# Three of sixteen output projection blocks as 32-bit products and as narrower halves in a streaming encoder layer

## The chip, the cores and the metric

The kernel runs on one core of a Trainium2 chip. The metric is the device time of one execution in microseconds (us). Before the change it is 1701.15 us, the median of three runs (1701.06 to 1701.47).

The engines of the core that matter here are TensorE (PE, matmuls; its weight loads have a row of their own, PEld), VectorE (DVE), ScalarE (ACT), GpSimd (POOL) and SyncE (SP), whose queue issues the loads from memory.

## The reference: what is computed

One layer of a streaming encoder for two request groups, 256 new positions of a prompt and 64 of a running stream, that share one set of weights. The two groups lie side by side as T = 320 columns, so each weight is read once. Cut to what matters:

```python
def layer(x, ...):                      # x: (B, T, 2048)
    xn = rmsnorm(x, norm_mix[l])
    proj = xn @ w_in[l]                 # q, k, v, u, vs, gates
    ...                                 # stick-breaking attention a, spatial gate bb
    gates = jax.nn.sigmoid(g + b_gate[l])
    g_a, g_b = gates[..., :D_MODEL], gates[..., D_MODEL:]
    merged = g_a * (a @ w_branch_a[l]) + g_b * (bb @ w_branch_b[l])
    h = x + merged @ w_out[l]           # the output projection: 2048 x 2048
    hn = rmsnorm(h, norm_ffn[l])
    gu = hn @ w_gate_up[l]
    h = h + (jax.nn.silu(gu[..., :D_FF]) * gu[..., D_FF:]) @ w_down[l]
    return h, k, v, vs
```

All inputs are 32-bit floats. The change touches `merged @ w_out` alone.

## The kernel before

Features lie on the 128 partitions and the 320 positions on the free axis. Each projection is cut into blocks of 128 output features. A block sums products over chunks of 128 input features into one accumulator `acc` in PSUM (three buffers), 128 x 320 of 32 bits.

**Products in halves.** Each 32-bit operand is kept as two tiles of the type `fp32r`: a high part, rounded, and a low part, the rest. For an activation these are pairs such as (`mh`, `ml`); for a weight they are `wh` and `wl`. `product` (lines 80 to 85) issues three matmuls for each 128 x 128 weight tile: high weight by high activation (L83), high weight by low activation (L84), low weight by high activation (L85), each over 320 columns. Each matmul has its own weight load.

**Weights.** `weights` (line 68) loads 128 x 1024 of a weight matrix (512 KB, eight tiles, half of a block with 16 tiles) into `raw` (three buffers) through SP's queue. ACT casts it to `wh` (L75), and DVE subtracts to get `wl` (L76); `wh` and `wl` have four buffers each. `block` (line 87) does this twice for an output block and issues 2 x 8 x 3 = 48 matmuls.

**The stage around the change.** The loop that merges the branches runs over m = 0 to 15. Its last round ends with the blocks of `w_a` and `w_b`; DVE multiplies them with the gates (L647, L649), adds them (L650), ACT casts the sum to `mh` (L653) and DVE subtracts to get `ml` (L654). The 16 pairs (`mh`, `ml`) are the list `merged`. Then the output projection runs over m = 0 to 15: a load of 128 x 320 of x into `xr` (two buffers, L662, kept in program order on SP), `block(w_out[m], merged)`, the residual add on DVE (L664, `h`), the scaled halves of the result for the next stage (L125 on ACT, L126 on DVE), and the sum of squares (ACT and POOL). The feed-forward stage follows.

**What sets the order.** Each engine works through its instructions in the order in which a scheduler put them when the program was built; DMAs of a queue are issued in order too. A tile's next use of a buffer waits until the last reader of the old content is done. The tag `B` has 32 buffers of 128 x 320. Up to the last round of the merge loop they hold the halves of both branches (`aT`, `bT`), and in the feed-forward stage the activations.

Products of full 32 bits, without halves, occur before the change only in the attention and gating parts, with 1, 64 or 128 columns: for instance L416 (128 columns), L488 (`wt` by `av` 128, `wt` by `cv` 64), L604 (128) and L728 (1 column). L418 and L488 with tiles `B` are products of halves over 256 columns, and L421 over 320. The first products, L243, are halves over 320 columns as well.

Of the kernel before, what the change touches and what calls it, by code (L numbers as in the profile page):

```python
# [8 lines left out]
F32 = mybir.dt.float32  # L9
F32R = mybir.dt.float32r  # L10
AF = mybir.ActivationFunctionType
ALU = mybir.AluOpType

P = 128
TP = 256
TS = 64
T = TP + TS
D = 2048
KD = D // P
H = 8  # L20
HALF = 8
# [12 lines left out]
def stream_step(ctx: ExitStack, tc: tile.TileContext, xT, w_in, w_a, w_b, w_out, w_gu, w_down,  # L34
                gains, ws_t, bs, ck_t, cv, y_t, k_t, v_t, sv_t):
    nc = tc.nc
    pool = lambda name, bufs=1, **kw: ctx.enter_context(tc.tile_pool(name=name, bufs=bufs, **kw))
    const = pool("const")
    wraw = pool("wraw", 3)
# [5 lines left out]
    def acc():  # L45
        return psum.tile([P, 512], F32, tag="acc", bufs=3, name="acc")
# [15 lines left out]
    def tick():  # L62
        state["tick"] += 1
        for fn, a in later.pop(state["tick"], ()):
            fn(*a)


    def weights(src, n, view=lambda t: t):
        raw = wraw.tile([P, HALF * P], F32, tag="raw", name="raw")
        d = nc.sync.dma_start(out=view(raw[:, : n * P]), in_=src)  # L70
        if state["tick"] < 4:
            tc.keep_in_program_order(d)
        wh = wsplit.tile([P, HALF * P], F32R, tag="wh", name="wh")
        wl = wsplit.tile([P, HALF * P], F32R, tag="wl", name="wl")
        nc.scalar.copy(out=wh[:, : n * P], in_=raw[:, : n * P])  # L75
        nc.vector.tensor_tensor(out=wl[:, : n * P], in0=raw[:, : n * P],  # L76
                                in1=wh[:, : n * P].bitcast(F32), op=ALU.subtract)
        return wh, wl

    def product(ps, w, j, x, first, last):  # L80
        wh, wl = w
        a, b = wh[:, j * P : (j + 1) * P], wl[:, j * P : (j + 1) * P]
        nc.tensor.matmul(ps[:, :T], a, x[0], start=first, stop=False, skip_group_check=True)  # L83
        nc.tensor.matmul(ps[:, :T], a, x[1], start=False, stop=False, skip_group_check=True)  # L84
        nc.tensor.matmul(ps[:, :T], b, x[0], start=False, stop=last, skip_group_check=True)  # L85

    def block(src, act, on=None):

        ps = acc()
        nk = len(act)  # L90
        if on is not None:
            nc.scalar.copy(out=ps[:, :T], in_=on)
        for k0 in range(0, nk, HALF):
            n = min(HALF, nk - k0)
            w = weights(src[:, k0 * P : (k0 + n) * P], n)
            for j in range(n):
                product(ps, w, j, act[k0 + j], on is None and k0 + j == 0, k0 + j == nk - 1)
            tick()
        return ps[:, :T]

    def slot(tag):
        return big.tile([P, T], F32R, tag=tag, bufs=32, name=tag)

    def pair(name):
        return big.tile([P, 2 * T], F32, tag="D", bufs=8, name=name)

    def halves(n, name):

        out, both = [], []
        for i in range(n):  # L110
            if i % 2 == 0:
                t = pair(name)
                both.append(t)
            out.append(t[:, i % 2 * T : (i % 2 + 1) * T])
        return out, both
# [7 lines left out]
    def gained(tag, src, gain):  # L123
        hi, lo = slot(tag), slot(tag)
        nc.scalar.activation(out=hi, in_=src, func=AF.Copy, scale=gain)  # L125
        nc.vector.scalar_tensor_tensor(out=lo, in0=src, scalar=gain, in1=hi.bitcast(F32),  # L126
                                       op0=ALU.mult, op1=ALU.subtract)
        return hi, lo

    def t320(tag, bufs=2, dt=F32):  # L130
        return tmp.tile([P, T], dt, tag=tag, bufs=bufs, name=tag)
# [429 lines left out]
    for g in range(H):  # L561
        ps = block(w_in[4 * H + g], xs)
        t = t320("ev")
# [60 lines left out]
    for g in range(H):  # L624
        ps = block(w_in[3 * H + g], xs)
        t = t320("ev")
# [5 lines left out]
    merged = []  # L632
    for m in range(KD):
        gate = []
        for i in range(2):
            ps = block(w_in[5 * H + i * KD + m], xs)
            t = t320("ev")
# [7 lines left out]
        ps = block(w_a[m], [aT[h] for h in range(H)])  # L645
        t = t320("mg", 1)
        nc.vector.tensor_tensor(out=t, in0=ps, in1=gate[0], op=ALU.mult)  # L647
        ps = block(w_b[m], [bT[g] for g in range(H)])
        nc.vector.tensor_tensor(out=gate[1], in0=ps, in1=gate[1], op=ALU.mult)  # L649
        nc.vector.tensor_tensor(out=t, in0=t, in1=gate[1], op=ALU.add)  # L650
        hi = mpool.tile([P, T], F32R, tag="C", bufs=32, name="mh")
        lo = mpool.tile([P, T], F32R, tag="C", bufs=32, name="ml")
# [2 lines left out]
        merged.append((hi, lo))  # L655


    (hs, ypair), hg = halves(KD, "h"), []
    sq = Squares("sq_h")
    for m in range(KD):  # L660
        x = t320("xr")
        tc.keep_in_program_order(nc.sync.dma_start(out=x, in_=xT[:, m, :]))  # L662
        ps = block(w_out[m], merged)
        nc.vector.tensor_tensor(out=hs[m], in0=ps, in1=x, op=ALU.add)  # L664
        hg.append(gained("A", hs[m], g_ffn[:, m : m + 1]))
        sq.add(hs[m], nc.vector if m == KD - 1 else None)
# [10 lines left out]
    for s0, n in SLICES:  # L677
        act = []
# [21 lines left out]
        for m in range(KD):  # L700
            end = s0 + n == KF and m == KD - 1
            ps = block(w_down[m][:, s0 * P : (s0 + n) * P], act, hs[m] if end else None)
# [133 lines left out]
```

## Time and profile before

| what | value |
|---|---|
| median of three runs | 1701.15 us |
| span of the profiled execution | 1699.7 us |
| run time less that span | 1.45 us |
| bytes read from memory | 256.03 MB |
| weight chunks split (L75, L76) | 468 |
| output projection in the trace | about 646.3 to 759 us |

The span goes from the first to the last instruction of one profiled execution; the run time also holds what lies around it. How to read the views: the page gives each engine's busy time and the chain of waits, followed back from the last instruction. A matmul's duration in the trace reaches from its start to the end of its results and overlaps with the next, so what a matmul costs in a stream is not its duration but the distance from one start to the next; the pieces of the chain give that distance. A matmul on 32-bit tiles has two records in the trace (the 8 matmuls of L416 have 16), one on halves has one.

### The profile page before, as it was taken

To read this page: it belongs to the slowest core of one execution; us is meant where nothing else is said; L and a number is where in the kernel's file an instruction comes from. 1 tells how busy PE (TensorE), PEld (TensorE's weight loads), DVE (VectorE), ACT (ScalarE), POOL (GpSimd) and SP (SyncE) were. 2 spreads that over 40 slices of the span, in tenths; PEclk is the share of its full clock that TensorE was granted. 3 is DMA by queue.
4 is the path that set the end of the run, shared out by engine and by line. 5 is a ranking of instruction groups with operands and counts; after the bars stand their busy time and mean duration, and the time that the engine had idled before them with its cause. 6 is when DMAs were issued, how large, how long until landed. Compare 5 with 4: busy or idle time off the path is not lost.

```text
span 1699.7 us, 27466 instructions
## 1 busy us (share of the span) xinstructions
PE 1689.7 (99%) x11544; PEld 1688.7 (99%) x11544; DVE 878.5 (52%) x1149; ACT 674.1 (40%) x888; POOL 57.3 (3%) x78
## 2 busy tenths in 40 slices
PE   9999999999999999999999999999999999999997
PEld 9999999999999999999999999999999999999997
DVE  6677656544444445555444444444444444444454
ACT  6655555433333333443333333333333323333342
POOL 0301021000000000110000000000000000000000
PEclk9999999999999999999999999999999999999999
DMA  6676556444444445554444454444444444444443
GB/s 249 192 222 172 173 165 177 146 150 151 151 150 151 151 157 165 172 165 149 149 149 149 151 150 150 151 153 149 152 150 149 149 149 149 149 150 149 136 150 124
DMA packets 100507, 268.30 MB, mean 158 GB/s; under 512 B 28992, under 2 KB 35392, under 8 KB 100384
## 3 DMA queue, kind: packets, MB, share of 16 engines
q1 hardware_dynamic: 97936, 261.36, 49.2%
q0 software_dynamic: 1312, 3.80, 0.6%
q8 instruction: 90, 1.47, 0.4%
q10 hardware_dynamic: 1136, 1.39, 0.2%
q14 instruction: 33, 0.27, 0.0%
HBM read 256.03 MB, written 5.51 MB: 154 GB/s over the span
## 4 chain that ended last, share of the span: by engine, by line
PE 99%; DMA 0%; DVE 0%; SPq 0%; ACT 0%; issue 0%; DVEq 0%
PE acc L83 32%; PE acc L85 32%; PE acc L84 32%; PE aux L243 2%; PE acc L243 1%; PE aux L488 1%; DMA raw<-w_in 0%; DVE h L760 0%; PE aux L604 0%; PE aux L418 0%; PE aux L421 0%; PE aux L416 0%; PE aux L728 0%; SPq L222 0%; PE aux L602 0%; ACT wh L233 0%
## 5 line engine op out<-in xcount | busy, mean ns | idle before, releaser
L75 ACT CAST wh<-raw 128x1024 fp32r<-128x1024 f32 x468 | 484.3, 1036 | 921.4 <-PE acc L84 742.7
L76 DVE TENSOR_TENSOR wl<-raw,wh 128x1024 fp32r<-128x1024 f32 x468 | 564.7, 1207 | 476.7 <-ACT wh L75 474.1
L83 PE MATMUL acc<-A,wh 128*128 128x320 f32 x2464 | 762.0, 309 | 0.0
L85 PE MATMUL acc<-A,wl 128*128 128x320 f32 x2464 | 761.4, 309 | 0.0
L84 PE MATMUL acc<-A,wh 128*128 128x320 f32 x2464 | 761.4, 309 | 0.0
L83 PEld LDWEIGHTS acc<-A,wh 128*128 128x128 f32 x2464 | 462.6, 188 | 0.0
L84 PEld LDWEIGHTS acc<-A,wh 128*128 128x128 f32 x2464 | 462.6, 188 | 0.0
L85 PEld LDWEIGHTS acc<-A,wl 128*128 128x128 f32 x2464 | 462.6, 188 | 0.0
L83 PE MATMUL acc<-B,wh 128*128 128x320 f32 x960 | 296.6, 309 | 0.0
L84 PE MATMUL acc<-B,wh 128*128 128x320 f32 x960 | 296.6, 309 | 0.0
L85 PE MATMUL acc<-B,wl 128*128 128x320 f32 x960 | 296.6, 309 | 0.0
L83 PEld LDWEIGHTS acc<-B,wh 128*128 128x128 f32 x960 | 180.2, 188 | 0.0
L84 PEld LDWEIGHTS acc<-B,wh 128*128 128x128 f32 x960 | 180.2, 188 | 0.0
L85 PEld LDWEIGHTS acc<-B,wl 128*128 128x128 f32 x960 | 180.2, 188 | 0.0
L83 PE MATMUL acc<-mh,wh 128*128 128x320 f32 x256 | 79.1, 309 | 0.0
L84 PE MATMUL acc<-ml,wh 128*128 128x320 f32 x256 | 79.1, 309 | 0.0
L85 PE MATMUL acc<-mh,wl 128*128 128x320 f32 x256 | 79.1, 309 | 0.0
L683 DVE TENSOR_TENSOR ev<-acc,rh 128x320 f32<-128x320 f32 x44 | 21.6, 491 | 56.6 <-PE acc L85 56.6
L686 DVE TENSOR_TENSOR bb<-acc,rh 128x320 f32<-128x320 f32 x44 | 21.6, 491 | 56.5 <-PE acc L85 56.5
L83 PEld LDWEIGHTS acc<-mh,wh 128*128 128x128 f32 x256 | 48.1, 188 | 0.0
L84 PEld LDWEIGHTS acc<-ml,wh 128*128 128x128 f32 x256 | 48.1, 188 | 0.0
L85 PEld LDWEIGHTS acc<-mh,wl 128*128 128x128 f32 x256 | 48.1, 188 | 0.0
(173 smaller groups left out, 727.5 us busy)
## 6 DMA issues: line engine op xcount, KB each, us to landing
raw<-w_gu SPq DMA_DIRECT2D x176, 512.0 KB, 3.6
raw<-w_in SPq DMA_DIRECT2D x141, 512.0 KB, 3.7
raw<-w_down SPq DMA_DIRECT2D x80, 512.0 KB, 3.5
raw<-w_out SPq DMA_DIRECT2D x32, 512.0 KB, 3.6
raw<-w_a SPq DMA_DIRECT2D x16, 512.0 KB, 3.5
raw<-w_b SPq DMA_DIRECT2D x16, 512.0 KB, 3.5
raw<-w_down SPq DMA_DIRECT2D x16, 256.0 KB, 2.7
x<-xT SPq DMA_DIRECT2D x8, 320.0 KB, 8.1
```

What stands on the lines that cost most here:

```text
L75: nc.scalar.copy(out=wh[:, : n * P], in_=raw[:, : n * P])
L76: nc.vector.tensor_tensor(out=wl[:, : n * P], in0=raw[:, : n * P], in1=wh[:, : n * P].bitcast(F32), op=ALU.subtract)
L83: nc.tensor.matmul(ps[:, :T], a, x[0], start=first, stop=False, skip_group_check=True)
L84: nc.tensor.matmul(ps[:, :T], a, x[1], start=False, stop=False, skip_group_check=True)
L85: nc.tensor.matmul(ps[:, :T], b, x[0], start=False, stop=last, skip_group_check=True)
L243: nc.tensor.matmul(first[b][h][:, :T], w[:, (h * n + j) * P : (h * n + j + 1) * P], xs[c + j][i], start=not last and c + j + i == 0, stop= ...
L488: mm = lambda out, a, b, first, last: nc.tensor.matmul(out, a, b, start=first, stop=last, skip_group_check=True)
L683: nc.vector.tensor_tensor(out=t, in0=pg, in1=got["rh"], op=ALU.mult)
L686: nc.vector.tensor_tensor(out=u, in0=pu, in1=got["rh"], op=ALU.mult)
```

## The change

After the merge loop, DVE adds each pair of halves back to a 32-bit tile: 16 adds of 128 x 320 (L661 of the changed kernel) into `B` buffers, the list `whole`. Then three of the sixteen output blocks take another form:

- m = 4: `whole_block` with one cut of 320 columns. The weight chunks are not split; the matmuls (L671) read `raw` and `whole` as 32-bit tiles, 16 of them, each over 320 columns.
- m = 8: the same with two cuts of 160 columns: 32 matmuls on 32-bit tiles, each over 160 columns.
- m = 12: `cut_block`, halves as before, but the product with the low weight part (L687) is issued as two matmuls of 160 columns each: 16 x (2 over 320 + 2 over 160).

The other thirteen blocks are as before.

```diff
+    whole = []
+    for hi, lo in merged:
+        t = slot("B").bitcast(F32)
+        nc.vector.tensor_tensor(out=t, in0=hi.bitcast(F32), in1=lo.bitcast(F32), op=ALU.add)
+        whole.append(t)
+
+    def whole_block(src, act, cuts):
+        ps = acc()
+        for k0 in range(0, len(act), HALF):
+            raw = wraw.tile([P, HALF * P], F32, tag="raw", name="raw")
+            nc.sync.dma_start(out=raw, in_=src[:, k0 * P : (k0 + HALF) * P])
+            for j in range(HALF):
+                for c in cuts:
+                    nc.tensor.matmul(ps[:, c], raw[:, j * P : (j + 1) * P], act[k0 + j][:, c],
+                                     start=k0 + j == 0 and c.start == 0, stop=k0 + j == KD - 1,
+                                     skip_group_check=True)
+            tick()
+        return ps[:, :T]
+
+    def cut_block(src, act):
+        ps = acc()
+        for k0 in range(0, len(act), HALF):
+            wh, wl = weights(src[:, k0 * P : (k0 + HALF) * P], HALF)
+            for j in range(HALF):
+                a, b = (t[:, j * P : (j + 1) * P] for t in (wh, wl))
+                for i in range(2):
+                    nc.tensor.matmul(ps[:, :T], a, act[k0 + j][i], start=k0 + j + i == 0, stop=False,
+                                     skip_group_check=True)
+                for c in (slice(0, T // 2), slice(T // 2, T)):
+                    nc.tensor.matmul(ps[:, c], b, act[k0 + j][0][:, c], start=False, stop=k0 + j == KD - 1,
+                                     skip_group_check=True)
+            tick()
+        return ps[:, :T]
+
+    CUTS = {4: (slice(0, T),), 8: (slice(0, T // 2), slice(T // 2, T))}
     (hs, ypair), hg = halves(KD, "h"), []
     sq = Squares("sq_h")
     for m in range(KD):
         x = t320("xr")
         tc.keep_in_program_order(nc.sync.dma_start(out=x, in_=xT[:, m, :]))
-        ps = block(w_out[m], merged)
+        ps = whole_block(w_out[m], whole, CUTS[m]) if m in CUTS else (cut_block if m == 12 else block)(w_out[m], merged)
```

What stands in each engine's program is seen at three places. Line numbers from 655 on differ between the two kernels (L664 becomes L699, L662 becomes L697). First PE, in the changed kernel, at the three blocks: the end of block 3 and block 4, then block 8, then the first step of block 12.

```order
L85 MATMUL acc<-mh,wl 128x320
L671 MATMUL acc<-B,raw 128x320 x16
L83 MATMUL acc<-mh,wh 128x320
...
L671 MATMUL acc<-B,raw 128x160 x32
...
L684 MATMUL acc<-mh,wh 128x320
L684 MATMUL acc<-ml,wh 128x320
L687 MATMUL acc<-mh,wl 128x160 x2
```

Before, each of these places has the 48 rows L83, L84, L85 in turn; now 16, 32 and 64 matmuls stand there.

Second DVE, at the end of the merge loop (a piece of the difference; `ev` belongs to the last gate, `mg` and `gate` to the last merge, and the `wl` rows are splits of the first chunks of `w_out`).

```order
 L76 TENSOR_TENSOR wl<-raw,wh 128x1024 x2
 L638 TENSOR_TENSOR ev<-acc,rx 128x320
-L76 TENSOR_TENSOR wl<-raw,wh 128x1024
+L661 TENSOR_TENSOR B<-mh,ml 128x320 x8
 L647 TENSOR_TENSOR mg<-acc,gate_6625 128x320
+L661 TENSOR_TENSOR B<-mh,ml 128x320 x7
 L76 TENSOR_TENSOR wl<-raw,wh 128x1024
 L649 TENSOR_TENSOR gate_6690<-acc,gate_6690 128x320
+L76 TENSOR_TENSOR wl<-raw,wh 128x1024
 L650 TENSOR_TENSOR mg<-mg,gate_6690 128x320
 L76 TENSOR_TENSOR wl<-raw,wh 128x1024
 L654 TENSOR_TENSOR ml<-mg,mh 128x320
```

Fifteen of the sixteen adds now stand between the last gate and the last merge, and the split of the second chunk of `w_out[0]` has moved behind them; the sixteenth add stands right behind `ml`. The first eight adds wait each for a matmul of the last block of `w_a` (steps 0 to 3), which frees the buffer that they write.

Third SP's queue around the loads for blocks 5 to 8, before and then after (`raw` are weight chunks, `xr` slices of x; what a row waits for stands behind it).

```order
L662 DMA xr_7053<-xT 128x320 [waits DMAHW6_49,DVE_49]
L70 DMA raw_7198<-w_out 128x1024 [waits DMAHW0_49,DVE_49]
L70 DMA raw_7228<-w_out 128x1024 [waits DMAHW2_49,DVE_49]
L662 DMA xr_7124<-xT 128x320 [waits DMAHW1_49,DVE_49]
L70 DMA raw_7269<-w_out 128x1024 [waits DMAHW3_49,DVE_49]
```

```order
L697 DMA xr_7085<-xT 128x320 [waits DMAHW6_49,DVE_49]
L70 DMA raw_7190<-w_out 128x1024 [waits DMAHW3_49,DVE_49]
L697 DMA xr_7116<-xT 128x320 [waits DMAHW1_49,DVE_49]
L70 DMA raw_7220<-w_out 128x1024 [waits DMAHW7_49,PE_49]
L70 DMA raw_7261<-w_out 128x1024 [waits DMAHW5_49,DMAHW0_49,DVE_49]
L70 DMA raw_7291<-w_out 128x1024 [waits PE_49]
L668 DMA raw_7332<-w_out 128x1024 [waits DMAHW7_49,DVE_49]
```

Before, every chunk waits for the split that frees its buffer (DVE). Now the chunks `raw_7220` (second half of block 6) and `raw_7291` (second half of block 7) wait for PE, since block 4 holds its two `raw` buffers until its matmuls have read them.

## The prediction

> **What bounds the kernel now.** I read the page first, then the chain of waits around the products of other widths, then single lines and the timeline of DVE.
>
> ```profile
> span 1699.7 us, 27466 instructions
> PE 1689.7 (99%) x11544; PEld 1688.7 (99%) x11544; DVE 878.5 (52%) x1149; ACT 674.1 (40%) x888; POOL 57.3 (3%) x78
> PEclk9999999999999999999999999999999999999999
> PE 99%; DMA 0%; DVE 0%; SPq 0%; ACT 0%; issue 0%; DVEq 0%
> ```
>
> PE is busy for 99% of the span, at full granted clock in all forty slices, and the chain that ended last is PE for 99%. A busy PE alone proves little, since matmuls overlap, but the chain says that hardly anything is waited for. So the change is worth what it adds to or takes from PE's stream in three blocks, plus any wait that it makes. DVE at 52% and ACT at 40% have room on average.
>
> What one block costs is read from DVE's timeline at the end of the merge loop:
>
> ```profile
> 636.83 1.23 DVE L76 TENSOR_TENSOR wl<-raw,wh 128x1024 fp32r<-128x1024 f32 x1 [2.29 <-ACT wh L75]
> 639.36 0.49 DVE L638 TENSOR_TENSOR ev<-acc,rx 128x320 f32<-128x320 f32 x1 [1.31 <-PE acc L85]
> 640.35 1.23 DVE L76 TENSOR_TENSOR wl<-raw,wh 128x1024 fp32r<-128x1024 f32 x1 [0.49 <-ACT wh L75]
> 642.88 0.49 DVE L647 TENSOR_TENSOR mg<-acc,gate 128x320 f32<-128x320 f32 x1 [1.31 <-PE acc L85]
> 646.40 0.49 DVE L649 TENSOR_TENSOR gate<-acc,gate 128x320 f32<-128x320 f32 x1 [1.31 <-PE acc L85]
> 646.93 0.49 DVE L650 TENSOR_TENSOR mg<-mg,gate 128x320 f32<-128x320 f32 x1
> 647.38 1.23 DVE L76 TENSOR_TENSOR wl<-raw,wh 128x1024 fp32r<-128x1024 f32 x1
> 653.44 0.49 DVE L664 TENSOR_TENSOR h<-acc,xr 128x320 f32<-128x320 f32 x1 [1.31 <-PE acc L85]
> ```
>
> DVE waits for the end of the last `w_b` block until 646.40 and for the end of output block 0 until 653.44. A block of 48 matmuls thus takes 7.04 us, 0.1467 us for each matmul over 320 columns.
>
> **What a product of another width or type costs.** The chain lists PE's pieces with their share of time; the attention's first products stand between ordinary ones:
>
> ```profile
> 62.62 0.22 PE aux L416 x2
> 62.84 0.36 PE aux L418 x3
> 63.79 0.58 PE aux L421 x4
> 279.59 0.89 PE aux L604 x8
> ```
>
> Halves over 256 columns (L418) cost 0.12 us each, over 320 (L421) 0.145, or 0.1467 in the long stream. The difference, 0.0267 us for 64 columns, is 0.417 ns a column; 320 columns stream for 0.1333 us, and 0.0133 us is left as a fixed part. A record of a 32-bit product over 128 columns (L416, L604) costs 0.89 / 8 = 0.111 us, and each such matmul has two records. Whether that 0.111 us is the stream or the weight load is told by the durations (minimum, median, maximum in ns):
>
> ```profile
> L728 PE MATMUL aux<-share,sq_f x6: 166/234/250, 1688.1 to 1689.0; 128*128 128x1 f32 x4, 128*64 128x1 f32 x2
> L488 PE MATMUL aux<-wt,cv x32: 222/275/275, 115.5 to 246.2; 128*128 128x64 f32 x32
> L416 PE MATMUL aux<-k,q x16: 270/273/274, 62.5 to 192.6; 128*128 128x128 f32 x16
> L418 PE MATMUL aux<-B x24: 281/285/365, 62.6 to 193.0; 128*128 128x256 f32 x24
> L243 PE MATMUL acc<-A,wh x64: 307/309/417, 5.3 to 40.0; 128*128 128x320 f32 x64
> ```
>
> The shortest 32-bit records grow from 166 to 270 ns over 127 columns, 0.82 ns a column. Halves grow from 281 to 309 over 64 columns, 0.44. So a 32-bit record streams its columns at half the pace, and there are two of them: four streams for each 32-bit product against one for a product of halves. I take 2 x 0.417 = 0.833 ns a column. Ends of matmuls are modelled, so a second sign is wanted; the timeline of PE, cut at two places, has it:
>
> ```profile
> 115.45 0.22 PE L488 MATMUL aux<-wt,cv 128*128 128x64 f32 x1
> 115.45 0.33 PE L488 MATMUL aux<-wt,cv 128*128 128x64 f32 x2
> ```
>
> Two records end 0.33 us after the first began, and the second lasts 0.275, so it began 0.055 us behind the first: 64 columns at 0.833 ns are 0.053. The weight load is seen in L243: its longest record, 417 ns, starts with its load in the open and is 0.108 us longer than the usual 309. The 0.111 us of a 128-column record is then both, 0.1067 us of stream with at most 0.0046 beside it, and a load of about that length.
>
> **The change, part by part.** Each block is set against its 7.04 us.
>
> Block 4, 32 records of 320 columns: 320 x 0.833 = 266.7 ns, plus the 4.6 ns left over at 128 columns: 0.2713 us each, 8.68 us in all, **+1.64**. The load (0.11) is hidden below the stream. No 32-bit record in the trace is wider than 128, so the fixed part is bounded: nothing (8.53 us, +1.49) to the 13.3 ns that halves pay (8.96, +1.92).
>
> Block 8, 64 records of 160 columns: 133.3 + 4.6 = 137.9 ns, still above the load: 8.83 us, **+1.79**. By the same bounds 8.53 to 9.39, +1.49 to +2.35.
>
> Block 12: the 32 matmuls over 320 columns stay, 4.69 us. The 16 low-weight products become 32 over 160. No row has halves under 256 columns. Their stream would be 66.7 ns, but each brings its own load of 0.108 to 0.111 us, and a load starts only as the product before it does, as the timelines of PE and PEld show:
>
> ```profile
> 800.06 0.31 PE L85 MATMUL acc<-A,wl 128*128 128x320 f32 x1
> 800.06 0.19 PEld L83 LDWEIGHTS acc<-A,wh 128*128 128x128 f32 x1
> ```
>
> I take 0.111: 3.56 us, block 8.25, **+1.21**. Bounds: 0.080 (stream and fixed part, load hidden; 2.56, +0.21) and 0.276 (as a 32-bit product of that width, two records of 0.138; 8.82, +6.48). I choose 0.111 because the 64- and 128-column records lie there, where two quite different streams give the same distance.
>
> The sixteen adds are 16 x 0.49 = 7.9 us of DVE, cost on the path: nothing, if they fit. Four chunks are no longer split, which frees DVE and ACT and gains nothing on a path that is PE. By the order, the first eight adds wait for steps 0 to 3 of the last `w_a` block, which ends at about 642.8, so the first buffer comes free near 639.9, when `ev` is done too. At 0.49 us each: eight adds to 643.8, `mg` to 644.3, seven adds to 647.7, the split of chunk 2 of block 0 (1.23) to 648.9. PE wants that at 646.30 + 3.52 + 0.29 = 650.1, a margin of 1.2 us. Behind it stand the gate product (649.4), a split (650.7), the add (651.2), another split (652.4) and `ml` (652.9); PE wants `ml` for the last step of block 0 at 653.05. That margin is only 0.2 us, but independent DVE instructions overlap (the split at 647.38 starts 0.45 us behind an add of 0.49), which over twenty of them gains most of a microsecond, so I take nothing for it. If the adds came only after the whole `w_a` block, the two waits would sum to about 2.9 us.
>
> Block 4 keeps two of three `raw` buffers until PE has read them, so SP's chunk for the second half of block 6 waits for half of block 4, and `xr` loads stand behind it.
>
> ```profile
> raw<-w_out SPq DMA_DIRECT2D x32, 512.0 KB, 3.6
> L75 ACT CAST wh<-raw 128x1024 fp32r<-128x1024 f32 x468 | 484.3, 1036 | 921.4 <-PE acc L84 742.7
> L76 DVE TENSOR_TENSOR wl<-raw,wh 128x1024 fp32r<-128x1024 f32 x468 | 564.7, 1207 | 476.7 <-ACT wh L75 474.1
> ```
>
> From its issue the chunk needs 3.6 + 1.04 + 1.21, about 5.9 us. It is issued 4.3 us into block 4 and used 8.68 + 7.04 + 3.52 = 19.2 us into it: 9 us to spare. Behind the waiting split on DVE stands the residual add of block 4, which frees one of three accumulators; that isn't wanted before block 7. So it costs nothing.
>
> The sum is 1.64 + 1.79 + 1.21 = **+4.64 us**. The profiled span goes from 1699.7 to 1704.3; the runs lie 1.45 us above the span, and I keep that: 1701.15 + 4.64 = **1705.8 us**. With all low bounds of this case (no fixed part, load 0.108) it is +4.1, with the high ones (13.3 ns, load 0.120) +5.8: 1705.2 to 1706.9.
>
> **Rivals.**
> 1. *The narrow halves product runs at the 32-bit pace* (0.276 us). For it: the kernel never issues halves under 256 columns and uses 32-bit products there. Against: the built program has one matmul instruction for it and two for a 32-bit one, and 0.111 us explains that choice as well. Time: 1.64 + 1.79 + 6.48 = +9.9, 1711.1 us.
> 2. *Its load is hidden* (0.080 us): +0.21 in block 12, in all +3.6, 1704.8 us; with no fixed part either, 1704.3. Against it: records of 64 columns stream for 0.053 us and still follow each other at 0.111.
> 3. *Not slower: a 32-bit record streams one column at the pace of halves*, and its durations are only modelled. Then block 4 is 32 x 0.1467 = 4.69 (-2.35), block 8 load-bound, 64 x 0.111 = 7.10 (+0.06), block 12 as forecast: -1.1, 1700.1 us. The sum changes sign at about 0.55 ns a column; I read 0.82.
> 4. *The adds come late* and PE waits for the second `wl` and for `ml`: +2.9 on top, 1708.7 us.
>
> On rival 2, the Trainium skill ("TensorE: Matmul & The Clock Gate", Back-to-back issue gap) gives about 81 ns for each load and matmul at 128 columns and 131 at 512; an estimate from that page for 160 columns is 85 ns, by which block 12 would cost +0.4 and the sum be +3.8. With that rule the trace disagrees, since its 128-column records lie at 111 ns. The same page (LDWEIGHTS) puts a load of 128 columns at 107 ns, and with that the trace's 0.108 agrees.
>
> **How the numbers follow.** Chances: forecast 0.66, narrow products slow 0.17, load hidden 0.07, not slower 0.05, adds late 0.05. Forecast, hidden load and late adds hold 0.78, short of 8 in 10, so the range has to reach to the slow narrow products: 1704.3 to 1711.6. A measurement of this kernel tells about 0.2% from no change, here 3.4 us, that is 1704.55. Above it lie the forecast, rivals 1 and 4 and half of rival 2: slower 0.91, same 0.08, faster 0.01.
>
> **What would show it right or wrong.** In the changed profile, L671 should stand at 0.271 us a record in block 4 and 0.138 in block 8, and L687 at 0.111; each block's length is read between the waits of DVE's residual adds (L699): 8.7, 8.8 and 8.25 us. PE should show no wait for `wl` or `mh` near 650 and 653 us. I am wrong if L687 lies near 0.08 or 0.28, if L671 shows a weight load or a fixed part that I didn't see at 128 columns, or if PE's idle time grows.

## The result, and the profile after

The changed kernel takes 1705.36 us (median of ten runs, 1705.3 to 1705.76); the kernel before, run beside it, 1701.05 us. The ratio is 1.0026, 95% interval 1.0016 to 1.0035: 4.31 us slower. The forecast was 1705.8 us, +4.64.

The page of the changed kernel: its span, busy times, granted clock and the chain that ended last.

```profile
span 1703.5 us, 27502 instructions
PE 1693.9 (99%) x11560; PEld 1690.8 (99%) x11560; DVE 876.7 (51%) x1161; ACT 670.4 (39%) x884; POOL 56.5 (3%) x78
PEclk9999999999999999999999999999999999999999
PE 99%; DVE 0%; DVEq 0%; issue 0%
```

PE is still the chain, at full clock, and has 4.2 us more of busy time (1693.9 against 1689.7). Nothing else became the bound. So the extra time should stand inside the three blocks. The chain of the changed kernel, in order of time (start, length, what), gives their ends: the first piece of block 4 and the first after it, the same for block 8, the same for block 12.

```profile
673.90 2.15 PE acc L671 x8
...
682.51 0.14 PE acc L83
...
703.62 1.63 PE acc L671 x12
...
712.32 0.14 PE acc L83
...
733.43 0.29 PE acc L684 x2
...
741.66 0.18 PE acc L83
```

Block 4 lasts 8.61 us, block 8 8.70, block 12 8.23, against 7.04 each: +1.57, +1.66 and +1.19, in sum +4.42. A further 0.03 us stands in the row at 741.66: the first product behind block 12 takes 0.18 instead of 0.15, because its weight load starts only with the last narrow product. The measured +4.31 is that sum within the scatter of the runs. (The spans of the two profiles differ by 3.8 us; in the profile of before the whole stream lies 0.6 us later already ahead of the change, as the rows of L638 at 639.36 and, below, at 638.74 show.)

The timeline of PE, first in block 4, then in block 8, then in block 12:

```profile
674.27 2.05 PE L671 MATMUL acc<-B,raw 128*128 128x320 f32 x7
...
704.82 1.39 PE L671 MATMUL acc<-B,raw 128*128 128x160 f32 x9
...
734.26 0.35 PE L684 MATMUL acc<-mh,wh 128*128 128x320 f32 x1
734.45 0.31 PE L684 MATMUL acc<-ml,wh 128*128 128x320 f32 x1
734.60 0.35 PE L687 MATMUL acc<-mh,wl 128*128 128x160 f32 x2
734.78 0.35 PE L684 MATMUL acc<-mh,wh 128*128 128x320 f32 x1
```

Seven records of 320 columns span 2.05 us, the last one lasting 0.432: (2.05 - 0.432) / 6 = 0.270 us from start to start, and over the block 8.61 / 32 = 0.269. Nine of 160 columns, the last one 0.299: (1.39 - 0.299) / 8 = 0.136. A step of block 12 goes from 734.26 to 734.78, 0.52 us; over the block it is (8.23 + 0.03) / 16 = 0.516. Two wide products at 0.1467 leave 0.223 us for the two narrow ones, 0.111 each. That is read over a whole step, because the single starts are uneven: the first wide product of the next step begins early, 0.19 us ahead of the second.

DVE at the end of the merge loop, in the changed kernel:

```profile
638.74 0.49 DVE L638 TENSOR_TENSOR ev<-acc,rx 128x320 f32<-128x320 f32 x1 [1.31 <-PE acc L85]
639.14 3.29 DVE L661 TENSOR_TENSOR B<-mh,ml 128x320 f32<-128x320 f32 x8
642.36 0.49 DVE L647 TENSOR_TENSOR mg<-acc,gate 128x320 f32<-128x320 f32 x1
642.76 2.89 DVE L661 TENSOR_TENSOR B<-mh,ml 128x320 f32<-128x320 f32 x7
645.57 1.22 DVE L76 TENSOR_TENSOR wl<-raw,wh 128x1024 fp32r<-128x1024 f32 x1
...
649.78 0.48 DVE L654 TENSOR_TENSOR ml<-mg,mh 128x320 fp32r<-128x320 f32 x1
```

The adds start right behind `ev`, 0.40 us apart. The split is done at 646.8 and `ml` at 650.3. Counted from `ev`, which marks the end of a block near 638.7, PE wants them near 649.5 and 652.4. The margins are 2.7 and 2.1 us, and the views of waits show no wait of PE or of its loads near them.

### The profile page after: what moved, and what is told of

Read it like the earlier page. It is cut to its first block, busy times and chain, and to the rows that moved or that the text cites. A ratio compares the mean times of both kernels' runs of the same rounds, so it can differ in the third digit from the quotient of the medians.

```text
span 1703.5 us, 27502 instructions
## 1 busy us (share of the span) xinstructions
PE 1693.9 (99%) x11560; PEld 1690.8 (99%) x11560; DVE 876.7 (51%) x1161; ACT 670.4 (39%) x884; POOL 56.5 (3%) x78
## 3 DMA queue, kind: packets, MB, share of 16 engines
q10 hardware_dynamic: 1136, 1.39, 0.2%
## 4 chain that ended last, share of the span: by engine, by line
PE 99%; DVE 0%; DVEq 0%; issue 0%
PE acc L85 31%; PE acc L84 31%; PE acc L83 31%; PE aux L243 2%; PE acc L671 1%; PE acc L243 1%; PE aux L488 1%; PE acc L684 0%; DVE h L795 0%; PE aux L214 0%; PE aux L604 0%; PE acc L687 0%; PE aux L418 0%; PE aux L421 0%; PE aux L416 0%; PE aux L763 0%
## 5 line engine op out<-in xcount | busy, mean ns | idle before, releaser
L83 PE MATMUL acc<-A,wh 128*128 128x320 f32 x2464 | 762.0, 309 | 0.0
L85 PE MATMUL acc<-A,wl 128*128 128x320 f32 x2464 | 761.4, 309 | 0.0
L84 PE MATMUL acc<-A,wh 128*128 128x320 f32 x2464 | 761.3, 309 | 0.0
L83 PEld LDWEIGHTS acc<-A,wh 128*128 128x128 f32 x2464 | 462.5, 188 | 0.0
L84 PEld LDWEIGHTS acc<-A,wh 128*128 128x128 f32 x2464 | 462.5, 188 | 0.0
L85 PEld LDWEIGHTS acc<-A,wl 128*128 128x128 f32 x2464 | 462.5, 188 | 0.0
L83 PE MATMUL acc<-B,wh 128*128 128x320 f32 x960 | 296.6, 309 | 0.0
L84 PE MATMUL acc<-B,wh 128*128 128x320 f32 x960 | 296.6, 309 | 0.0
L85 PE MATMUL acc<-B,wl 128*128 128x320 f32 x960 | 296.6, 309 | 0.0
L83 PEld LDWEIGHTS acc<-B,wh 128*128 128x128 f32 x960 | 180.2, 188 | 0.0
L84 PEld LDWEIGHTS acc<-B,wh 128*128 128x128 f32 x960 | 180.2, 188 | 0.0
L85 PEld LDWEIGHTS acc<-B,wl 128*128 128x128 f32 x960 | 180.2, 188 | 0.0
L83 PE MATMUL acc<-mh,wh 128*128 128x320 f32 x208 | 64.6, 311 | 0.0
L84 PE MATMUL acc<-ml,wh 128*128 128x320 f32 x208 | 64.3, 309 | 0.0
L85 PE MATMUL acc<-mh,wl 128*128 128x320 f32 x208 | 64.3, 309 | 0.0
L742 DVE TENSOR_TENSOR h<-acc,h 128x320 f32<-128x320 f32 x47 | 23.0, 489 | 46.4 <-PE acc L85 46.4
L83 PEld LDWEIGHTS acc<-mh,wh 128*128 128x128 f32 x208 | 39.0, 188 | 0.1
L84 PEld LDWEIGHTS acc<-ml,wh 128*128 128x128 f32 x208 | 39.0, 188 | 0.1
```

The costliest lines, as they stand in the source:

```text
L742: nc.vector.tensor_tensor(out=hs[m], in0=ps, in1=hs[m], op=ALU.add)
```

## Experiments

Three blocks give 1.2 to 1.7 us each, only a few times a scatter of 0.3. So each form was first made in twelve blocks, m = 4 to 15, alone. Below, "over before" is the difference of medians against runs of the kernel before on the same chip.

**Twelve blocks as 32-bit products over 320 columns.**

```diff
-    CUTS = {4: (slice(0, T),), 8: (slice(0, T // 2), slice(T // 2, T))}
+    CUTS = {m: (slice(0, T),) for m in range(4, KD)}
...
+        ps = whole_block(w_out[m], whole, CUTS[m]) if m in CUTS else block(w_out[m], merged)
```

> Blocks 4 to 15 (twelve) all as 32-bit products over 320 columns. If block 4 of the change cost what its 32 records show (0.269 us each, 8.61 us against 7.04), twelve of them cost +18.8 us over the kernel before. Rival: the fixed part is the 4.6 ns of my forecast, +19.7. Rival: the change's block was cheap only because its loads had been prefetched and twelve in a row, each holding raw buffers until PE has read them, run into waits for loads: well above +20, with PE idle before L671.

Measured: 1719.93 us, +18.96 over before (ratio 1.0111, interval 1.0096 to 1.0126). That is 12 x 1.58, where block 4 of the change gave 1.57. No wait for loads appears, although twelve such blocks in a row hold their raw buffers: all records of the twelve follow each other at 268 to 270 ns.

**Twelve blocks over 2 x 160 columns.** The same edit with `(slice(0, T // 2), slice(T // 2, T))`.

> Blocks 4 to 15 all as 32-bit products over 2 x 160 columns. From 0.1357 us a record, 64 records: 8.68 us a block, +1.64 each, +19.7 us over before; the weight load (0.111) hides below the stream of 0.136. With my forecast's fixed part 12 x 1.79 = +21.5. Rival (waits for loads): above that, with PE idle.

Measured: 1721.12 us, +20.15 (ratio 1.0118, interval 1.0104 to 1.0132), between the two sums. In its trace the records follow each other at 135 or 136 ns, 0.1358 on the mean, which gives 12 x 1.65 = +19.8 and leaves 0.35 us, about the scatter.

**Twelve blocks with the low-weight product in two.** No `whole`, no adds.

```diff
-        ps = whole_block(...) if m in CUTS else (cut_block if m == 12 else block)(w_out[m], merged)
+        ps = (cut_block if m >= 4 else block)(w_out[m], merged)
```

> Blocks 4 to 15 all in halves with the low-weight product over 2 x 160 columns, no 32-bit tiles and no adds. If each narrow product is bound by its weight load (0.111 us): 16 x (2 x 0.1467 + 2 x 0.1116) = 8.27 us a block, +1.2 each, +14.7 us over before. Rival, load hidden (0.080): +2.5. Rival, 32-bit pace: +78.

Measured: 1715.57 us, +14.60 (ratio 1.0086, interval 1.0072 to 1.0100). This is the load's price and neither of the rivals', which lie 12 us below and 63 above.

**The adds alone.**

```diff
-        ps = whole_block(...) if m in CUTS else (cut_block if m == 12 else block)(w_out[m], merged)
+        ps = block(w_out[m], merged)
```

> Only the sixteen adds, whose tiles nobody reads; all sixteen blocks as before. My theory: hidden, 0.0 us (within 0.3). Rival: the 6.5 us of DVE work at the end of the merge loop delays the split of the second chunk or the last low half and PE waits: +0.5 to +2.9 us, with a wait of PE near 650 us.

Measured: 1701.29 against 1700.97 us (ratio 1.0001, interval 0.9993 to 1.0010). No change that can be measured, and no wait of PE near 650 us.

The next runs ask why a narrow product of halves costs 0.111 us.

**Cut at 256 instead of 160.** As the third run, with `(slice(0, TP), slice(TP, T))`, that is 256 and 64 columns.

> As a3, but the low-weight product is cut into 256 + 64 columns. Bound by the load where the stream is shorter: 0.120 (256 columns) + 0.111 (64 columns) = 0.231 us a step, 8.39 us a block, twelve blocks +16.2 us over before. Rival: a further product of halves costs a fixed extra whatever the widths: the same as a3, +14.7.

Measured: 1717.47 us, +16.43 (ratio 1.0097, interval 1.0082 to 1.0112). So the extra depends on where the cut lies, as it must if a product costs the longer of its stream and its load. A fixed price for a further product would have given 1.7 us less. The step in the timeline:

```profile
700.78 0.31 PE L681 MATMUL acc<-mh,wl 128*128 128x256 f32 x2
700.93 0.39 PE L678 MATMUL acc<-mh,wh 128*128 128x320 f32 x1
701.16 0.31 PE L678 MATMUL acc<-ml,wh 128*128 128x320 f32 x1
701.30 0.31 PE L681 MATMUL acc<-mh,wl 128*128 128x256 f32 x2
```

The row of L681 joins the 256- and the 64-column product; both have begun and a wide one has started 0.15 us later. That wide record then lasts 0.39 instead of 0.31 us: it has started early and stands until its weights are there. The price of the 64-column product is paid in the record behind it.

**A shorter load.**

```diff
-                    nc.tensor.matmul(ps[:, c], b, act[k0 + j][0][:, c], ...)
+                    nc.tensor.matmul(ps[: P // 2, c], b[:, : P // 2], act[k0 + j][0][:, c], ...)
```

> As a3, but the two low-weight products over 160 columns load only 64 of the 128 weight columns and write 64 of 128 output rows; the low-weight product of the other 64 outputs of blocks 4 to 15 is left out. If the narrow product waits for the next load: the first is followed by a short load (0.055) and costs its own stream, 0.080, the second is followed by a full load and costs 0.111: 7.75 us a block, +8.5 us over before. Rival: 0.111 is a floor of a narrow product whatever its load: +14.7 as a3. Rival: the stream alone counts: +2.5.

Measured: 1707.30 us, +6.26 (ratio 1.0038, interval 1.0025 to 1.0051). A floor of 0.111 for a narrow product is ruled out (+14.7), and so is the stream alone (+2.5). My own number was 2.2 us too high. One step of its chain, two wide products and two narrow, and then the rows of a step in the timeline:

```profile
700.86 0.32 PE acc L678 x2
701.18 0.15 PE acc L681 x2
701.33 0.33 PE acc L678 x2
...
700.22 0.34 PE L678 MATMUL acc<-mh,wh 128*128 128x320 f32 x1
700.40 0.30 PE L678 MATMUL acc<-ml,wh 128*128 128x320 f32 x1
700.54 0.31 PE L681 MATMUL acc<-mh,wl 128*64 128x160 f32 x2
700.69 0.34 PE L678 MATMUL acc<-mh,wh 128*128 128x320 f32 x1
```

The narrow pair takes 0.15 us, 0.074 from start to start, where I had taken 0.080 for the first. The two wide ones take 0.183 and 0.142: the first waits for a full load behind the second narrow product, and the second, which has a short load beside it, is 0.005 faster than usual. Twelve blocks of 16 steps of 0.473 us make +6.3. The run halves the output rows of the narrow products too, but that isn't what makes them cheap: the second one also writes 64 rows, and with a full load behind it it still costs 0.074 + 0.183 - 0.147 = 0.110 us, the excess being paid in the record behind it.

**A still shorter load.** The same with 32 weight columns (`P // 4`), to see whether the fixed part follows the length of the load.

> As b2, with 32 of 128 weight columns in the low-weight products of blocks 4 to 15; the low-weight product of the other 96 outputs is left out. In b2 a product of halves followed by a load of 64 columns cost 142 ns (320 columns) and 74 ns (160), a fixed part of 8 ns where 128-column loads leave 13. Theory: the fixed part goes with the columns of the load that runs beside the product, so here about 5.5: 139 and 72 ns, 7.49 us a block, +5.4 us over before. Rival: the fixed part is one of two values and stays at 8: the time of b2, +6.3.

Measured: 1707.70 us, +6.65 (ratio 1.0038, interval 1.0025 to 1.0052). That theory fell, and the rival held: the time is that of the half load or slightly more. The first narrow product starts 140 to 147 ns behind the wide one ahead of it, and the starts behind narrow products are mostly 74 ns on. What sets the fixed part is open.

The last runs are on the sum and on the cover of the adds.

**Without the third part.** Block 12 as before, the rest as in the change.

> The change without its third part: block 12 in halves over 320 columns as before; blocks 4 and 8 in 32 bits, adds as in the change. By the records: 1.57 + 1.64 = +3.2 us over before, 1.2 less than the change. Rival: the parts don't add up (the cost of block 12 is hidden or is paid elsewhere): the change's +4.3 or as low as +2.5.

Measured: 1704.21 us, +3.16 (ratio 1.0019, interval 1.0010 to 1.0028), 1.15 us below the change. The parts add up.

**Every add twice.**

```diff
+        for _ in range(2):
-        nc.vector.tensor_tensor(out=t, in0=hi.bitcast(F32), in1=lo.bitcast(F32), op=ALU.add)
+            nc.vector.tensor_tensor(out=t, in0=hi.bitcast(F32), in1=lo.bitcast(F32), op=ALU.add)
```

> The change with every one of the sixteen adds issued twice (same result). By the order, the split of the second chunk of output block 0 then stands behind 32 adds. From the 0.403 us between adds it ends near 654.9 us on the changed kernel's clock, where PE wants it at 649.5: PE waits some 5.3 us, so +5.3 over the change, +9.6 over before. Rival: DVE is only half busy and 6.5 us more are hidden: the time of the change, +4.3.

Measured: 1712.66 us, +11.62 (ratio 1.0069, interval 1.0053 to 1.0086). The wait came where it was expected, and the run cost 2 us more than that. The view of PE's waits and the chain of this kernel:

```profile
PE acc L85 <- DVE wl L76: 5.0, 1, 5.0
...
653.53 1.15 DVE wl L76
654.67 0.04 issue
654.72 0.63 PE acc L85
655.35 0.27 PE acc L83
...
658.82 0.27 PE acc L84
659.09 0.23 PE acc L85
659.31 0.15 PE acc L83
```

PE waited 5.0 us for the second split. From 655.35 to 659.09 fourteen products follow at 0.267 us instead of 0.147, and then the stream is at full pace again. The granted clock, the share of full speed that PE was given, is 0.79 between 655 and 665 us. In the row it stands behind the busy times of PE, PEld, DVE, ACT and POOL:

```profile
655.00:665.00 10.00, 10.00 (x56) 10.00 (x57) 5.68 (x7) 3.86 (x5) 0.00 (x0) 0.79 0.69 226
```

The same view in narrower windows has the clock at 1.00 until 652.3 us, at 0.50 from there to 659.1, and at 1.00 behind it. Fourteen times 0.12 us, and the slow start ahead of them, are the missing 2 us.

**Seven adds twice.** The same with `range(2 if 8 <= len(whole) < 15 else 1)`, for a shorter wait.

> The change with seven of the sixteen adds issued twice (same result). By the order, 23 adds and the four instructions of the last merge stand ahead of the second split of output block 0; at 0.403 us each the split starts near 650.1 us, and PE waits about 1.9 us. Theory: the 7.3 us that doubling all adds cost above the change were a wait of 5.3 and then 2.0 of matmuls at half clock, which only a wait of that length brings; with 1.9 us of wait the next matmuls follow at 0.147 and the kernel costs +1.9 over the change, +6.2 over before. Rival: after any wait the stream is slow for a while (or the late loads cost again): some products at 0.267, +7 or more over before.

Measured: 1707.38 us, +6.33 (ratio 1.0037, interval 1.0023 to 1.0050), 2.0 above the change. The waits and the chain:

```profile
PE acc L85 <- DVE wl L76: 1.4, 1, 1.4
...
649.98 1.15 DVE wl L76
651.13 0.04 issue
651.17 0.42 PE acc L85
651.59 0.14 PE acc L83
651.73 0.14 PE acc L84
```

With a wait of 1.4 us in the records the next products follow at full pace, and the granted clock is 1.00 throughout. The wait is paid once. It costs somewhat more than the 1.4 us: from the last start ahead of it, at 649.44, to the second one behind it, at 651.42, are 1.98 us instead of 0.29, that is 1.7 us lost. The rest of the 2.0 is within the scatter.

## Why the prediction was right, by its own steps

- **The bound.** PE's stream is all that counts in this stage. That held: the time changed by what the three blocks add, and by nothing else beyond the scatter.
- **Block 4**, forecast 8.68 us, measured 8.61. The pace of 0.833 ns a column, read from records of at most 128 columns, held at 320. The fixed part was mis-sized: I took the 4.6 ns that 128-column records leave above their stream, and it is 8.61 / 32 - 0.2667 us, 2.4 ns. The 128-column records, whose distance is that of their load, showed an upper bound and not the value.
- **Block 8**, forecast 8.83 us, measured 8.70: the same mis-sizing, 64 times instead of 32. Together the two make 0.2 us of the 0.33 by which the forecast was high; the rest is within the scatter of the runs.
- **Block 12**, forecast 8.25 us, measured 8.23. A narrow product costs its load; the cut at 256 and the short load show that it is the load and not the width. The Trainium skill ("TensorE: Matmul & The Clock Gate", Back-to-back issue gap) gives about 81 ns at 128 columns; by an estimate from that page, 85 ns at 160, the block would have cost +0.4. The trace shows +1.2 and decides.
- **The adds**, forecast to cost nothing, with margins of 1.2 and 0.2 us. The forecast of no cost held, but I had the adds 0.49 us apart, their duration, where they start 0.40 apart, and the margins are 2.7 and 2.1. The overlap of DVE instructions was named and taken at nothing. Sixteen more adds, 6.4 us, used the margins up, together with three instructions of the last merge (L649, L650, L654) that stood ahead of the split in that order.
- **The loads** held back by block 4: hidden, as worked out; twelve such blocks in a row showed no wait either.
- **The rivals.** Narrow products at 32-bit pace would have shown records at 0.276 us, which aren't there. The hidden load fell with the step of 0.52 us. A 32-bit stream at the pace of halves fell with 0.270. Late adds didn't happen; my price for them was the wait alone, and the wait of 5.0 us, when it was made, cost about 2 us more than itself.

None of the forms beats three products of halves over 320 columns: at 7.04 us a block, that form is the shortest of the four.

## What to carry to other kernels

Read a product's price from the distance between starts, over a whole step where a record can start ahead of its weights. Ask for each width whether the stream or the weight load sets it. Here a load of 128 columns is 0.111 us, and products of halves over 160 and over 64 columns both cost about that. By an estimate from these figures, (111 - 13.3) / 0.417, the load sets the price under some 235 columns; no run lies between 160 and 256. Cutting one product of 320 columns in two cost 0.076 us at 160 + 160 and 0.086 us at 256 + 64 (the +14.60 and +16.43 us over 192 cut products).

A 32-bit product is two records at half pace, 2 x 0.269 us over 320 columns, so three products of halves at 3 x 0.147 are cheaper there. That doesn't carry to narrow ones: over 160 columns a 32-bit product is 2 x 0.136 = 0.272 us, and three products of halves, each held by its load, would by estimate be 3 x 0.111 = 0.333. No run here cuts all three.

Work on an engine that is half idle is free only up to the margin at its place in the order, and that margin is counted from instruction starts, not durations: here 2.7 us, which sixteen adds fit into, and 23 of them with the last merge do not.

## What the runs showed that was not expected

- A wait of PE of 5.0 us was followed by fourteen products at 0.267 us before the stream returned to 0.147; a wait of 1.4 us was not. The granted clock fell to 0.50 at 652.3 us, 2.9 us after the start of the last product ahead of the wait (649.38), and was back at 1.00 at 659.1, 4.4 us after the first product behind the wait. The Trainium skill ("TensorE: Matmul & The Clock Gate", Part 1) says that the clock falls to half after an idle window of about 3.4 us and returns after a busy one of that length. That only the longer wait brought half clock agrees with it, and so does the return; the fall came after less idle time than the page's window.
- The fixed part beside the stream is 13.3 ns for a wide product of halves with a full load beside it, about 8 ns (142 - 133.3 and 74 - 66.7) with a load of 64 columns, no less on the mean with 32, and 2.4 ns for a 32-bit record. Why is open.
